# The sums along heads of a gated recurrence in two runs of five matmuls, and its last transposes twice as far apart in the plan

## The chip, the cores and the metric

The kernel runs on one core of a Trainium2 chip. A core has TensorE (PE in the profile, with its weight loads as PEld), VectorE (DVE), ScalarE (ACT), GpSimd (POOL) and SyncE (SP), which issues most of the DMAs. The metric is the device time of one execution in microseconds (us), as a median over runs.

## The reference

Two layers of a hybrid backbone are computed, one over 128 context rows and one over 512 latent rows, together 640 rows of 1024 features. Four token mixers work side by side: a short gated convolution, a gated recurrence in both directions (HGRN2), a neighbourhood attention and a chunked gMLP. A feed-forward net follows. The change touches the recurrence, which in the reference is this, for each head of 64 and for each direction:

```python
q, k, log_f, v = chunks(q), chunks(k), chunks(log_f), chunks(v)    # of 32 rows
cum = jnp.cumsum(log_f, axis=3)
rel = cum[:, :, :, :, None, :] - cum[:, :, :, None, :, :]
decay = jnp.exp(jnp.where(tri, rel, -jnp.inf))
scores = jnp.einsum('bhctd,bhcsd,bhctsd->bhcts', q, k, decay)
o_intra = jnp.einsum('bhcts,bhcsv->bhctv', scores, v)
...
def step(s, gu):
    g_c, u_c = gu
    return g_c[..., None] * s + u_c, s
s_last, s_in = lax.scan(step, s0, (g, u))
...
o = o_f + flip(o_b)
o = o * lax.rsqrt(jnp.mean(o * o, axis=-1, keepdims=True) + EPS)
return o * norm_g * silu(g), s_f, s_b
```

## The kernel before

The 640 rows are held with features along the 128 partitions. The main stream of the program is the projection of the input: for each output tile of 128 features, TensorE multiplies weights by the activations in three passes (high weight x high input, high x low, low x high). The lines are L362 (in `gemm_half`, 128x320 results) and L933 (in `tok_tile`, 128x256 results); the text calls their matmuls the main matmuls. The weights are split on the way: ACT copies the high part (L323), and DVE subtracts it from the raw weight for the low part (L324).

Everything else of the mixers runs beside that stream as jobs. A job is a Python generator that writes some instructions and then yields a number of planned microseconds. The main stream calls `tick(us)` after every three matmuls, which moves a planned clock on; each job whose due time has come then writes its next piece. `pe(us)` moves the planned clock without running a job. A yield is multiplied by the job's slack, 1.3 for the recurrence. So these numbers set where the job's matmuls stand between the main matmuls of TensorE. The framework's own scheduler then sets the order on each engine, by its estimate of when operands are there; so on DVE and ACT, and in places on TensorE, the order is not that of the code. Once fixed, each engine takes its instructions in that order.

The recurrence (`hgrn`) is computed by levels. `along` (L466) sums products over the features of a head by a matmul with a 128x2 matrix `heads`; ten such matmuls make the sums of the 640 rows and two halves, and it is called twice, once on `ksum` (in tile D) and once, at level 0, on `near` (in tile E). At each level from 1 to 6 rows are joined in blocks of twice the size:

- TensorE multiplies keys by queries in small matmuls (L526: 32x32 at levels 1 to 5, 64x64 at level 6). A level has two groups (`par` 0 and 1), at level 6 four; the queries `qq` are tile C, the keys are tile B (`kk`) or, up to level 4, copies of it in tile D or E (L493, L494).
- DVE takes the result into place under a mask (L531, up to level 4); at levels 5 and 6 ACT does it (L535). At level 4, ACT copies the four blocks of the whole to the final place (L541).
- DVE updates keys and queries with the gates: four multiplications (L545), two of tile B, then two of tile C, and one of the gates themselves (L549, tile A). The next level's matmuls read what these wrote.

After the levels the states are carried from tile to tile (L565, L574), the outputs are summed (L619 to L626) and normed (L610), and at the end they are transposed (L648), ten times in five pairs, and DVE multiplies each half by gains and gates (L652).

Other jobs in the same stretch are `gmlp`, whose norm goes by DVE (L304), GpSimd's power (L305) and five multiplications on DVE (L681); its matmuls are L686; and `ada_cols`, which makes modulation vectors on DVE (L262, two passes over 1024 elements per column, tiles H, X or A; then L228, L231 or L268).

Of the kernel before, what the change touches and what calls it, by code (L numbers as in the profile page):

```python
# [67 lines left out]
def tile_step(ctx: ExitStack, tc: tile.TileContext, a: dict, outs: list, dbg=None):  # L68
# [21 lines left out]
    def pe(us):  # L90
        now[0] += us
# [38 lines left out]
    def pm():  # L130
        return psm.tile([P, 512], F32, tag="m", name=nm("m"))
# [74 lines left out]
    for x in LORD.split():  # L206
        if x[0] == "w":
            i, h = int(x[1]), int(x[2])
# [238 lines left out]
    def hgrn():  # L447
# [13 lines left out]
        def along(x):  # L461

            m = pm()
            mv = m[:, 0:20].rearrange("p (r i) -> p i r", r=2)
            for i in range(10):
                mm(mv[:, i, :], x[:, i * P:(i + 1) * P], heads, start=True, stop=True)  # L466
                pe(0.22)
                yield 0.5
            return m


# [5 lines left out]
        for j in range(2):  # L477
            vec.tensor_tensor(n2[:, j], k2(j)[:, j], q2(1 - j)[:, 1 - j], ALU.mult)
        dm = yield from along(ksum)

        near_at = hd[:, 1280:1920].rearrange("p (r i t) -> p r i t", r=2, i=10)
# [17 lines left out]
        for l in range(7):  # L499
# [5 lines left out]
            if l == 0:  # L505
                m = yield from along(near)
                vec.copy_predicated(nat, lmask[:, 0, :].unsqueeze(1).to_broadcast([P, 20, 32]), bc(m))
# [137 lines left out]
        for t in range(5):  # L645
            m = pm()
            for pr in range(2):
                ten.transpose(m[:, pr * P:(pr + 1) * P],  # L648
                                    og[:, t * 256 + pr * P:t * 256 + (pr + 1) * P], ident)
                pe(0.11)  # L650
                s = sg[:, pr * T + t * P:pr * T + (t + 1) * P]
                vec.scalar_tensor_tensor(s, m[:, pr * P:(pr + 1) * P],  # L652
                                         p1[:, C_HN + pr:C_HN + pr + 1], s, ALU.mult, ALU.mult)
            yield 0.4
        nc.sync.dma_start(ybd, split_y("D", sg).bitcast(F32))
        R["hgrn_done"] = True
        R["yd"] = split_y("E", R["yt"])
# [1 line left out]
    def split_y(tag, y):  # L659
        w = region(tag, [P, 2, 2, T], F32R)  # L660
        wf = w.rearrange("p h k t -> p h (k t)")
        act(wf[:, 0], y, AF.Copy)
        vec.tensor_tensor(wf[:, 1], y, wf[:, 0].bitcast(F32), ALU.subtract)
        return w
# [233 lines left out]

    SLACK = {"q": 1.3, "du": 1.4, "ax": 1.0, "cv": 1.1}
    starts = {"q": hgrn, "du": gmlp, "ax": conva, "cv": attn}  # L900

    def in_tile(sec, n, w):
# [1318 lines left out]
```

## Time and profile before

| | us |
|---|---|
| median of 3 runs | 1024.82 |
| lowest and highest | 1024.57, 1025.02 |
| the profiled execution | 1023.97 |
| its span on the core | 1022.1 |
| TensorE busy | 1008.3 (99%) |
| DVE busy | 790.1 (77%) |
| ACT busy | 538.6 (53%) |
| POOL busy | 106.5 (10%) |

The profile is of one execution, and its times are microseconds from the start of the span. A row of the timeline gives start, duration, engine, line, operation, output and inputs by the names of their tiles, shapes and a count; in brackets stands the idle time of the engine just before it and what ended that. A row of waits gives who waited for whom: the sum, the number of times and the longest. A row of a window gives its length and the busy time of PE, PEld, DVE, ACT and POOL, each with a count, then the granted clock of TensorE, the share of DMA and GB/s. "x2" behind a MATMUL counts the passes that the hardware makes of an instruction on 4-byte data, two each.

### The profile page before, as it was taken

How to read it: one execution, taken by the hardware profiler on the slowest of the kernel's cores; microseconds unless marked ns; L12 is line 12 of the kernel's file. 1: busy time of each engine (PE TensorE's matmuls, PEld its weight loads, DVE VectorE, ACT ScalarE, POOL GpSimd, SP SyncE). 2: the span in 40 equal slices, each digit the busy share in tenths (PEclk: the TensorE clock that was granted, in tenths of full speed). 3: DMA queues.
4: the chain of work that ended last, by engine and by line, in shares of the span. 5: the costliest groups of instructions: out<-in, count | busy, mean ns of one | idle time of the engine just before them, and what ended most of it. 6: DMA issues, size and time to landing. Idle time of an engine off the chain costs nothing.

```text
span 1022.1 us, 18764 instructions
## 1 busy us (share of the span) xinstructions
PE 1008.3 (99%) x7572; PEld 951.9 (93%) x7572; DVE 790.1 (77%) x1308; ACT 538.6 (53%) x933; POOL 106.5 (10%) x153
## 2 busy tenths in 40 slices
PE   8999999999999999999999999999999999999997
PEld 6899999999899999999998899999999999888886
DVE  6758899769866676767868879998888887796644
ACT  6642343354555444444544567777777776634432
POOL 1000020312100000000010111111112221001101
PEclk9999999999999999999999999999999999999999
DMA  9864433597562413323179584765555669974212
GB/s 354 322 221 127 126 124 114 171 263 216 143 206 79 155 52 104 130 77 104 49 282 349 207 328 112 195 163 150 150 151 149 154 161 271 370 259 146 83 42 103
DMA packets 55926, 177.85 MB, mean 174 GB/s; under 512 B 8192, under 2 KB 14624, under 8 KB 53280
## 3 DMA queue, kind: packets, MB, share of 16 engines
q1 hardware_dynamic: 45008, 140.60, 39.6%
q0 software_dynamic: 10832, 36.06, 14.8%
q8 instruction: 59, 0.97, 0.4%
q14 instruction: 27, 0.22, 0.1%
HBM read 134.93 MB, written 25.46 MB: 157 GB/s over the span
## 4 chain that ended last, share of the span: by engine, by line
PE 91%; DVE 5%; DMA 1%; issue 1%; ACT 1%; POOL 1%; SPq 0%; POOLq 0%; DVEq 0%; ACTq 0%
PE g L1478 19%; PE m L1122 17%; PE g L362 14%; PE g L1813 8%; PE m L1813 6%; PE g L1135 5%; PE m L1478 4%; PE m L1262 3%; PE g L933 2%; PE g L1262 2%; PE m L148 2%; PE g L148 1%; PE m L1473 1%; PE m L526 1%; DMA A<-in_w_ada_dram 1%
## 5 line engine op out<-in xcount | busy, mean ns | idle before, releaser
L362 PE MATMUL g<-XH,w 128*128 128x320 f32 x704 | 171.4, 317 | 0.0
L362 PEld LDWEIGHTS g<-XH,w 128*128 128x128 f32 x704 | 120.6, 188 | 2.4 <-issue 1.2
L362 PE MATMUL g<-XL,w 128*128 128x320 f32 x352 | 108.8, 309 | 0.0
L362 PEld LDWEIGHTS g<-XL,w 128*128 128x128 f32 x352 | 66.3, 188 | 0.0
L311 DVE TENSOR_TENSOR w<-raw,w 128x1024 fp32r<-128x1024 f32 x34 | 41.4, 1221 | 14.9 <-ACT w L310 9.1
L1122 PE MATMUL m<-XH,w 128*128 128x320 f32 x224 | 52.5, 309 | 0.0
L1813 PE MATMUL g<-w,XH 128*128 128x512 f32 (+1 forms) x216 | 50.2, 385 | 0.0
L1813 PEld LDWEIGHTS g<-w,XH 128*128 128x128 f32 x216 | 39.5, 188 | 8.3 <-ACT XH L1772 0.3
L310 ACT ACTIVATE w<-raw 128x1024 fp32r<-128x1024 f32 x34 | 35.7, 1050 | 21.3 <-PE g L1262 10.0
L1813 PE MATMUL g<-w,XL 128*128 128x512 f32 (+1 forms) x180 | 42.4, 386 | 0.0
L148 DVE SCALAR_TENSOR_TENSOR X<-MG,p2t,X 128x641 f32<-128x641 f32 x44 | 38.9, 885 | 4.3 <-ACT X L148 3.4
L148 DVE SCALAR_TENSOR_TENSOR X<-X,p2t,X 128x641 f32<-128x641 f32 x44 | 38.9, 884 | 1.9 <-ACT X L148 1.0
L1813 PEld LDWEIGHTS g<-w,XL 128*128 128x128 f32 x180 | 33.4, 188 | 7.1 <-DVE dt L1828 0.2
L148 ACT ACTIVATE w<-raw 128x1024 fp32r<-128x1024 f32 (+3 forms) x46 | 38.2, 851 | 2.7 <-DMA raw<-in_w_in_dram 1.7
L1478 PE MATMUL g<-XL,w 128*128 128x320 f32 x240 | 38.6, 310 | 0.0
L1478 PE MATMUL g<-XL,C 128*128 128x320 f32 x240 | 38.4, 309 | 0.0
L1122 PEld LDWEIGHTS m<-XH,w 128*128 128x128 f32 x224 | 38.3, 188 | 0.0
L1478 PEld LDWEIGHTS g<-XL,w 128*128 128x128 f32 x240 | 36.0, 188 | 0.5 <-ACT MG L148 0.3
L1813 PE MATMUL m<-w,XH 128*128 128x512 f32 (+1 forms) x156 | 36.4, 381 | 0.0
L1478 PEld LDWEIGHTS g<-XL,C 128*128 128x128 f32 x240 | 35.9, 188 | 0.4 <-ACT MG L148 0.4
L1122 PE MATMUL m<-XL,w 128*128 128x320 f32 x112 | 34.6, 309 | 0.0
L1813 PEld LDWEIGHTS m<-w,XH 128*128 128x128 f32 x156 | 28.5, 188 | 5.6
(549 smaller groups left out, 2751.9 us busy)
## 6 DMA issues: line engine op xcount, KB each, us to landing
raw<-in_w_up_dram SPq DMA_DIRECT2D x30, 512.0 KB, 4.9
raw<-in_w_gp_dram SPq DMA_DIRECT2D x21, 640.0 KB, 4.0
raw<-in_w_down_dram SPq DMA_DIRECT2D x22, 512.0 KB, 4.0
raw<-in_w_in_dram SPq DMA_DIRECT2D x19, 512.0 KB, 4.2
H<-in_w_adt_dram SPq DMA_DIRECT2D x16, 512.0 KB, 4.5
actd<-X POOLq DMA_DIRECT2D x22, 320.5 KB, 5.4
X<-in_w_adt_dram SPq DMA_DIRECT2D x10, 512.0 KB, 4.0
upd<-XL SPq DMA_DIRECT2D x4, 1280.0 KB, 6.4
```

The costliest lines, as they stand in the source:

```text
L148: r = f(*args, **kw)
L310: act(w[0], raw, AF.Copy)
L311: vec.tensor_tensor(w[1], raw, w[0].bitcast(F32), ALU.subtract)
L362: mm(o, w[:, h, k0 + k, :], r(k)[:, s], start=(k == 0 and i == 0), stop=(k == kt - 1 and i == 2))
L526: mm(m[W * g:W * g + W, (i - s0) * W:(i - s0 + 1) * W], lhs, rhs, start=True, stop=True, tile_position=(64 * par, W * g))
L933: mm(o, x(kx)[:, ts], w[:, h, k, :], start=(kx == 0 and i == 0), stop=(kx == 7 and i == 2))
L1122: mm(o, w[:, k, :], x[:, k, :], start=(first and k == 0 and j == 0), stop=(k == 3 and j == 2), skip_group_check=True)
L1135: mm(pb[:, c, 0:HC], w[:, h + k, :], y[:, x, k, s], start=(k == 0 and j == 0), stop=(k == 1 and j == 2))
L1262: mm(m, mh[k // 2][:, hx, k % 2, t * P:(t + 1) * P], wo[q][:, hw, k % 2, :], start=(k == 0 and i == 0), stop=(k == 7 and i == 2))
L1473: mm(o, w[:, k, :], x[:, k, :], start=(first and not part and k == 0 and j == 0), stop=(part == 1 and k == 3), skip_group_check=True)
L1478: z = mm(o, w[:, k, :], x[:, k, :], start=(first and k == 0 and j == 0), stop=(k == 3 and j == 2), skip_group_check=True)
L1813: mm(ps, sl[k][hx][:, t * P:(t + 1) * P], w[:, hw, k, c0:c1], start=first, stop=end and (last or nh == 1 and t == 4 and kk_ == 7))
```

## The change

`along` yields after every fifth matmul, 2.5 planned us, and not after each, 0.5. The last transposes are 0.8 planned us apart in place of 0.4. Both are multiplied by the slack.

```diff
             for i in range(10):
                 mm(mv[:, i, :], x[:, i * P:(i + 1) * P], heads, start=True, stop=True)
                 pe(0.22)
-                yield 0.5
+                if i % 5 == 4:
+                    yield 2.5
             return m
...
                 vec.scalar_tensor_tensor(s, m[:, pr * P:(pr + 1) * P],
                                          p1[:, C_HN + pr:C_HN + pr + 1], s, ALU.mult, ALU.mult)
-            yield 0.4
+            yield 0.8
         nc.sync.dma_start(ybd, split_y("D", sg).bitcast(F32))
```

Behind L468 every line number is one higher in the changed kernel: L526 is its L527, L545 its L546 and so on. Each engine has the same instructions in both kernels. The order is the same up to the first call of `along` and again from about 223 us on; in between, it differs on every engine.

On TensorE, in the first call of `along`, the sums (L466) stand between main matmuls (L933). Before:

```order
L466 MATMUL m_1057<-heads,D_927 128x2
L933 MATMUL m_991<-w_873,XH_253 128x256 x2
L933 MATMUL m_991<-w_873,XL_15_254 128x256
L933 MATMUL m_991<-w_873,XH_253 128x256
L466 MATMUL m_1057<-heads,D_927 128x2
L933 MATMUL m_991<-w_873,XH_253 128x256
L933 MATMUL m_991<-w_873,XL_15_254 128x256
L933 MATMUL m_991<-w_873,XH_253 128x256
```

After, from the same place:

```order
L466 MATMUL m_1057<-heads,D_927 128x2 x5
L934 MATMUL m_991<-w_873,XH_253 128x256 x2
L934 MATMUL m_991<-w_873,XL_15_254 128x256
L934 MATMUL m_991<-w_873,XH_253 128x256 x2
L934 MATMUL m_991<-w_873,XL_15_254 128x256
```

The second run of five follows 19 main matmuls behind the first, and the tenth single of before 43 behind its first. In the second call the two runs stand behind 282 and 300 main matmuls, counted from the start; the ten singles stood behind 297 to 351.

On DVE, at level 4 and the updates of level 5 (128x40x16 is level 4, 128x20x32 is level 5). Before:

```order
L304 TENSOR_SCALAR dss<-dss 128x5
L545 TENSOR_TENSOR B_795<-B_795,A_794 128x40x16 x2
L681 TENSOR_SCALAR X_126_1318<-X_126_1318,dss 128x256 x2
...
L531 COPY_PREDICATED D_927<-lmask,m_1890 128x320
L545 TENSOR_TENSOR C_1008<-C_1008,A_794 128x40x16 x2
L549 TENSOR_TENSOR A_794<-A_794 128x80
L262 SCALAR_TENSOR_TENSOR junk_1942,ar_1943<-H_1529,S_94_1047 128x1024
L262 SCALAR_TENSOR_TENSOR junk_2050,ar_2051<-X_99_1078,S_94_1047 128x1024
L262 SCALAR_TENSOR_TENSOR H_1529,ar_1943<-H_1529,S_94_1047 128x1024
L324 TENSOR_TENSOR w_1964<-raw_1659,w_1964 128x1024
L228 TENSOR_SCALAR modt<-ar_1943,cst 128x2
L545 TENSOR_TENSOR B_795<-B_795,A_794 128x20x32 x2
L545 TENSOR_TENSOR C_1008<-C_1008,A_794 128x20x32 x2
```

After:

```order
L546 TENSOR_TENSOR B_795<-B_795,A_794 128x40x16
L304 TENSOR_SCALAR dss<-dss 128x5
L682 TENSOR_SCALAR X_124_1314<-X_124_1314,dss 128x256 x5
L532 COPY_PREDICATED D_927<-lmask,m_1842 128x320
L546 TENSOR_TENSOR C_1008<-C_1008,A_794 128x40x16 x2
L550 TENSOR_TENSOR A_794<-A_794 128x80
L324 TENSOR_TENSOR w_1897<-raw_1573,w_1897 128x1024
L262 SCALAR_TENSOR_TENSOR junk_1987,ar_1988<-H_1620,S_94_1047 128x1024
L262 SCALAR_TENSOR_TENSOR junk_2097,ar_2098<-X_97_1072,S_94_1047 128x1024
L262 SCALAR_TENSOR_TENSOR X_97_1072,ar_2098<-X_97_1072,S_94_1047 128x1024
L546 TENSOR_TENSOR B_795<-B_795,A_794 128x20x32 x2
L546 TENSOR_TENSOR C_1008<-C_1008,A_794 128x20x32 x2
```

The two updates of B that stood between L304 and the multiplications of L681 stand ahead of L304, and L324 stands ahead of three L262 and not behind them. On ACT the weight's high copy L323 stands behind the four copies L541 in both; the evacuation L412 between them has gone ahead of them.

On TensorE, from the last group of level 5 to the first of level 6, 30 main matmuls (L362) stand between before and 36 after. Before, the start and the end of that stretch (gmlp's L686 is in it):

```order
L526 MATMUL m_2056<-C_1008,B_795 32x32 x40
L362 MATMUL g_1969<-XH_253,w_1656 128x320
...
L686 MATMUL m_2156<-G_1983,X_126_1318 64x128 x4
L362 MATMUL g_2148<-XH_253,w_1804 128x320
L362 MATMUL g_2148<-XL_15_254,w_1804 128x320
L362 MATMUL g_2148<-XH_253,w_1804 128x320
L526 MATMUL m_2166<-C_1008,B_795 64x64 x10
```

After:

```order
L527 MATMUL m_1993<-C_1008,B_795 32x32 x40
L362 MATMUL g_1902<-XH_253,w_1570 128x320
...
L362 MATMUL g_2065<-XH_253,w_1747 128x320 x2
L362 MATMUL g_2065<-XL_16_255,w_1747 128x320
L362 MATMUL g_2065<-XH_253,w_1747 128x320
L527 MATMUL m_2106<-C_1008,B_795 64x64 x10
```

Counted from the start, the second group of level 5 stood behind 600 main matmuls and stands behind 564; the first group of level 6 stood behind 630 and stands behind 600.

The transposes L648 stood behind 822 to 840 main matmuls, at 825, 828 and 834 two at one place; they stand behind 777 to 809, at 801 two at one place. Around them on DVE, before (tile MG takes the transposes' results, D_ and E_ the split outputs):

```order
L663 TENSOR_TENSOR E_2728<-X_126_1318,E_2728 128x1280
L262 SCALAR_TENSOR_TENSOR junk_2737,ar_2738<-H_2497,S_94_1047 128x1024
L262 SCALAR_TENSOR_TENSOR H_2497,ar_2738<-H_2497,S_94_1047 128x1024
L231 TENSOR_SCALAR modt<-ar_2738,bada_240,cst 128x2
```

After, the first L652 (its L653) stands ahead of the first of these L262, and the second between the two:

```order
L653 SCALAR_TENSOR_TENSOR MG_113_1236<-m_2622,cst,MG_113_1236 128x128
L262 SCALAR_TENSOR_TENSOR junk_2746,ar_2747<-H_2554,S_94_1047 128x1024
L653 SCALAR_TENSOR_TENSOR MG_113_1236<-m_2622,cst,MG_113_1236 128x128
L653 SCALAR_TENSOR_TENSOR MG_113_1236<-m_2633,cst,MG_113_1236 128x128
L262 SCALAR_TENSOR_TENSOR H_2554,ar_2747<-H_2554,S_94_1047 128x1024
```

## The prediction

> **What bounds the kernel now.** I read the busy shares first, then the chain of work that ended last, then the waits of TensorE, then the timeline around the places that the new order touches.
>
> ```profile
> PE 1008.3 (99%) x7572; PEld 951.9 (93%) x7572; DVE 790.1 (77%) x1308; ACT 538.6 (53%) x933; POOL 106.5 (10%) x153
> PEclk9999999999999999999999999999999999999999
> PE 91%; DVE 5%; DMA 1%; issue 1%; ACT 1%; POOL 1%; SPq 0%; POOLq 0%; DVEq 0%; ACTq 0%
> PE g L148 <- DVE F L148: 1.6, 1, 1.6
> ...
> PE m L648 <- DVE MG L652: 1.0, 1, 1.0
> ```
>
> TensorE (PE) is busy 99% of the span, makes up 91% of the chain and is granted nine tenths of its clock or more in every slice. So a change pays only if it shortens the issue of TensorE or removes one of its waits, and it costs if it creates one. In the part of the program whose order changes, the only large wait is the last row: 1.0 us before a transposition of L648. VectorE (DVE) is busy 77%, but it is not idle evenly, and that is what decides below.
>
> The sum is made against the profiled execution, 1023.97 us, of which 1022.1 is the span. It lies 0.85 below the median of 1024.82, so I add the change to the median. What a measurement here can tell from no change is 0.2%, or 2.05 us.
>
> **Part 1: sums in runs of five.** No instruction is added or removed on any engine. Twenty matmuls of L466, two columns wide, stand as four runs of five. Each is cheap to compute, so what counts is how far it pushes the matmul behind it.
>
> ```profile
> 83.29 0.28 PE L466 MATMUL m<-heads,D 128*128 128x2 f32 x2
> ...
> 83.64 0.28 PE L933 MATMUL g<-w,XL 128*128 128x256 f32 x1
> 83.76 0.28 PE L933 MATMUL g<-w,XH 128*128 128x256 f32 x1
> 83.88 0.50 PE L466 MATMUL m<-heads,D 128*128 128x2 f32 x4
> ...
> 84.44 0.28 PE L933 MATMUL m<-w,XL 128*128 128x256 f32 x1
> ...
> 91.89 0.31 PE L362 MATMUL g<-XH,w 128*128 128x320 f32 x1
> 92.03 0.28 PE L466 MATMUL m<-heads,E 128*128 128x2 f32 x2
> 92.17 0.39 PE L362 MATMUL g<-XH,w 128*128 128x320 f32 x1
> 92.40 0.31 PE L362 MATMUL g<-XL,w 128*128 128x320 f32 x1
> ```
>
> Starts tell the cost. A matmul of L933 takes 0.12 (83.64 to 83.76). The single at 83.29 and its successor take 0.35 to 83.64, so the single costs 0.35 - 0.12 = 0.23. The pair at 83.88 costs 0.56 - 0.12 = 0.44, that is 0.21 for the second of it. Between matmuls of L362, which take 0.14 to 0.15, the single at 92.03 costs 0.37 - 0.15 = 0.22: 0.14 until the next starts, and 0.08 by which that next one is longer. Before, the order has two pairs and six singles in the first call of along and ten singles in the second: 0.88 + 1.38 + 2.2 = 4.5 us. After, each run costs 0.23 + 4 x 0.21 = 1.07, four of them 4.3. I take -0.1, since no run longer than two is in this trace. If the inner ones cost only the 0.14, sixteen of them save 16 x 0.08 = 1.3; if each costs what a single does, 20 x 0.23 = 4.6 make +0.1. So the bounds are -1.3 and +0.1, and the pair is the nearest row.
>
> **Part 2: the whole recurrence stands earlier.** This is the large part. Five single steps of 0.65 planned us are rounded up to the next call of tick, one step of 3.25 is rounded once. In the order that results, TensorE's steps of the recurrence come 30 to 51 main matmuls earlier at each of the levels. Counted in matmuls of L362 and L933 from the start, the first 64x64 matmuls of L526 (level 6) stand behind 630 before and behind 600 now. Behind 600 there stood before the second group of level 5:
>
> ```profile
> 145.40 0.89 PE L526 MATMUL m<-C,B 64*32 64x32 f32 x80
> 146.22 0.41 PE L362 MATMUL g<-XH,w 128*128 128x320 f32 x1
> ...
> 152.39 0.80 PE L526 MATMUL m<-C,B 64*64 64x64 f32 x20
> ```
>
> Up to that point TensorE has the same work in both orders, so it reaches the 64x64 matmuls at about 146.2 to 146.4 instead of 152.39. What they read are the two level-5 updates of C on DVE (L545). Does DVE come earlier too?
>
> ```profile
> DVE D L531 <- PE m L526: 3.0, 2, 2.2
> DVE B L545 <- PE m L526: 0.7, 1, 0.7
> DVE X L681 <- POOL dss L305: 0.3, 1, 0.3
> 105.30:149.30 44.00, 43.90 (x1049) 41.35 (x1048) 39.80 (x69) 17.96 (x37) 5.61 (x6) 1.00 0.39 122
> 105.36 1.23 DVE L324 TENSOR_TENSOR w<-raw,w 128x1024 fp32r<-128x1024 f32 x1 [1.65 <-ACT w L323]
> 132.82 0.15 DVE L304 TENSOR_SCALAR dss<-dss 128x5 f32<-128x5 f32 x1
> 132.94 1.56 DVE L545 TENSOR_TENSOR B<-B,A 128x640 f32<-128x640 f32 x2
> 134.83 0.62 DVE L681 TENSOR_SCALAR X<-X,dss 128x256 f32<-128x256 f32 x2 [0.33 <-POOL dss L305]
> 138.59 0.52 DVE L531 COPY_PREDICATED D<-lmask,m 128x320 f32<-128x320 uint8 x1 [0.79 <-PE m L526]
> 139.00 1.54 DVE L545 TENSOR_TENSOR C<-C,A 128x640 f32<-128x640 f32 x2
> 140.68 1.22 DVE L262 SCALAR_TENSOR_TENSOR junk<-H,S 128x1024 bf16<-128x1024 f32 x1
> 144.11 1.33 DVE L324 TENSOR_TENSOR w<-raw,w 128x1024 fp32r<-128x1024 f32 x1
> 146.32 1.56 DVE L545 TENSOR_TENSOR B<-B,A 128x640 f32<-128x640 f32 x2 [0.71 <-PE m L526]
> 147.80 1.55 DVE L545 TENSOR_TENSOR C<-C,A 128x640 f32<-128x640 f32 x2
> 133.05 1.75 POOL L305 TENSOR_TENSOR dss<-dss,neghalf 128x5 f32<-128x5 f32 x1 [81.91 <-DVE dss L304]
> 139.14 2.99 ACT L541 ACTIVATE MG<-D 32x640 f32<-32x640 f32 x4 [3.31 <-DVE D L531]
> ...
> 142.88 1.07 ACT L323 ACTIVATE w<-raw 128x1024 fp32r<-128x1024 f32 x1
> ```
>
> In the 44.0 us from L324 at 105.36 to the end of the level-5 updates, DVE is busy 39.8 (the third pair of the window's row) and idle about 4.0, by the three waits: 3.0 + 0.7 for TensorE and 0.3 for GpSimd (POOL). DVE's work in the stretch is nearly the same in the new order: one L262 more and one L324 less, 1.1 to 1.2 us each, and a small L228 or L268 less. With TensorE earlier, its 3.7 of idle go, and the levels would come 3.7 earlier, were there not two waits in their place:
> - L681 now stands directly behind L304. L304 hands to POOL's pow (133.05, 1.75), and L681 starts at 134.83, 1.89 after the 132.94 at which the next work could begin. Before, the two updates of B at 132.94 (1.5 together) lay in between, and 0.33 was left as a wait. In the new order both stand ahead of L304, and nothing is left in between: 1.6 more.
> - L324 now stands directly behind level 4's updates of C and L549; before, three L262 (140.68 to 144.11, 3.4) were in between. It needs L323 of ScalarE (ACT), which stands behind the four copies L541, and these wait for the second L531: 2.99 + 1.07 = 4.1 behind it. DVE has from 139.00 to 140.68 to do in that time, 1.7. So 2.1 to 2.4 idle, in place of none.
>
> Sum 1.9 + 2.1 to 2.4 = 4.0 to 4.3, against 4.0 before: DVE ends the two level-5 updates of C where it did, the second at 147.80 + 1.55 = 149.3, the first half of that span earlier, at 148.6. TensorE stands there from 146.2 or 146.4. It waits about 2.2 for the first and 0.6 for the second, 2.8 in all, and behind it in its queue stand main matmuls that need none of this. Before, the same data had 152.39 - 149.3 = 3.1 us to spare. Nothing later gives it back: TensorE has no idle time to shrink, and from 223 us on the orders are the same. Bounds: 0 if DVE's chain comes forward by 2.8 or more after all, and 4.4 if each of the two DVE waits comes out 0.8 longer. I take 2.8.
>
> The other levels have their L526 earlier too, but DVE's idle time before them (3.7) says that DVE waited for TensorE there. Small waits of 0.1 may appear at levels 2 to 4; I add 0.1.
>
> For the clock, the row of granted clock shows 9 in the slices that hold the waits of 1.6 and 1.0, so I take a wait of 2.8 at its own length. [...]
>
> **Part 3: the last transposes.** Spaced 1.04 planned us apart in place of 0.52, two of them no longer meet in one gap.
>
> ```profile
> 199.27 0.27 PE L648 MATMUL m<-cst,MG 128*128 128x128 f32 x1
> 200.56 0.33 PE L648 MATMUL m<-cst,MG 128*128 128x128 f32 x1 [1.02 <-DVE MG L652]
> ...
> 195.90 1.49 DVE L663 TENSOR_TENSOR E<-X,E 128x1280 fp32r<-128x1280 f32 x1
> ...
> 198.57 1.22 DVE L262 SCALAR_TENSOR_TENSOR H<-H,S 128x1024 f32<-128x1024 f32 x1
> 199.84 0.29 DVE L231 TENSOR_SCALAR modt<-ar,bada,cst 128x2 f32<-128x2 f32 x1
> 200.16 0.61 DVE L652 SCALAR_TENSOR_TENSOR MG<-m,cst,MG 128x128 f32<-128x128 f32 x2
> ```
>
> The second transposition waits 1.02 for L652, because DVE is in L663, two L262 and L231 until 200.16. In the new order the first L652 stands ahead of those L262, and more main matmuls stand between two transposes. I take 0.85 of the 1.02 as gone, with 0.1 to 0.2 left; bounds 0 and 1.0. The DMA behind the last L652 goes out earlier, and nobody waits for it here.
>
> **Sum:** -0.1 + 2.8 + 0.1 - 0.85 = +2.0 us (1.95). On the median, 1024.82 + 2.0 = 1026.8 us: a little slower, almost exactly at the 2.05 that can be told.
>
> **Rivals.**
> (a) The wait at level 6 does not come: DVE's chain moves forward with TensorE, because POOL's pow or ACT's L323 find other cover (the L324 buffer loaded earlier, or L304 issued earlier than I read). For it: DVE idled 3.7 for TensorE. Against it: the two rows of POOL and ACT above. It decides if no more than 1.2 of the two DVE waits is left (4.0 of idle less the 2.8 by which the chain must come forward). Then only L648's 0.85 and the 0.1 count: 1023.9.
> (b) The other side, faster: runs of five cost 0.14 for each inner matmul, -1.3, and the chain of DVE keeps up as in (a): -1.3 - 0.85 = -2.15, 1022.7. The point from which it counts as faster is 0.075 saved per inner matmul without any wait at level 6. Against it: the pair at 83.88, where the second cost 0.21.
> (c) More waits: TensorE is 30 to 51 matmuls of 0.15 (4.5 to 7.6 us) earlier at every level, and DVE turns out to be the bound at levels 3 or 4 as well, where L531 waited only 0.79. One more wait of 2 to 3: 1029.3.
> [...]
>
> **How the numbers follow.** My forecast (level 6 waits between 1.2 and 4, net +0.5 to +3.2) has 0.60, divided evenly by the bound at 2.05. (a) has 0.16, of it 0.03 on the faster side; (b) 0.12, (c) 0.09, (d) 0.03. So faster 0.15, same 0.30 + 0.13 = 0.43, slower 0.30 + 0.12 = 0.42. The range: at the low end (b) and part of (a) are left out, 1023.4, at the high end most of (c), 1028.6.
>
> **What the profile after would show.** Among TensorE's waits a new row, L527 (the old L526) on DVE's C, L546, 2 to 3 us in one or two pieces, and L649 on L653 below 0.3. On DVE a wait of L682 on POOL of 1.9 and of L324 on ACT's L323 of over 2, and nearly none on L527. Inside a run of five, starts of 0.2 apart. I am wrong if the wait at level 6 is missing or under 1 us, if the L324 directly behind L550 finds its L323 done, or if the starts inside a run are 0.14 apart.

## The result and the profile after

The changed kernel takes 1029.9 us (median of 5 runs, 1028.93 to 1034.62) against 1024.65, so by the medians it is 5.3 us slower. The ratio over all the runs, which two long ones raise, is 1.0066, with a 95% interval of 1.0051 to 1.0081. The forecast was 1026.8, with a range of 1023.4 to 1028.6.

The five runs fall into two groups: 1028.93, 1029.09 and 1029.9, and 1033.45 and 1034.62. The profiled execution is of the second group (1033.45 us, a span of 1031.6). Its page, in the rows that answer to those of before:

```profile
PE 1015.8 (98%) x7572; PEld 957.4 (93%) x7572; DVE 789.2 (77%) x1308; ACT 538.5 (52%) x933; POOL 112.1 (11%) x153
PEclk9999999999999999999999999999999999999999
PE 77%; issue 9%; DVE 6%; DMA 4%; ACT 1%; POOL 1%; SPq 0%; POOLq 0%; DVEq 0%; ACTq 0%
```

TensorE fell from 91% of the chain to 77%. "issue" went from 1% to 9%, and DVE and DMA gained 4 points together. The row of granted clock shows no dip, because a slice is 25.8 us long and the dip lies across two of them. A window of 15 us does. Its row, with the clock third from the end:

```profile
145.00:160.00 15.00, 13.73 (x120) 12.18 (x118) 10.83 (x19) 4.55 (x10) 0.97 (x1) 0.66 0.33 108
```

Windows of 1 us show 1.00 up to 149 us, 0.50 from 150 to 159 us and 1.00 from 160 us on, so a mean of 0.66 over 15 us is (1 - 0.66) x 15 / 0.5 = 10.2 us at half clock, and about 5 us are lost. The waits of TensorE between 76 and 240 us, and below them the timeline where the clock falls:

```profile
PE m L649 <- DVE MG L653: 2.2, 2, 1.3
PE m L527 <- DVE C L546: 1.3, 2, 0.9
PE g L934 <- issue: 0.2, 1, 0.2
```

```profile
147.00 0.31 PE L362 MATMUL g<-XH,w 128*128 128x320 f32 x1
148.17 0.33 PE L527 MATMUL m<-C,B 64*64 64x64 f32 x2 [0.86 <-DVE C L546]
148.91 0.79 PE L527 MATMUL m<-C,B 64*64 64x64 f32 x18 [0.41 <-DVE C L546]
149.63 0.63 PE L362 MATMUL g<-XH,w 128*128 128x320 f32 x1
```

The wait at level 6 is there (0.86 + 0.41 idle; by starts 0.93 + 0.63, about 1.6), and the first main matmul behind it takes 0.63 in place of 0.41. The transposes wait 2.2 us in place of 1.0. (By the counts of the traces, L466 and L527 have two rows for each matmul of the code, x20 for the ten of a call. Main matmuls and transposes have one, so there "x2" is two matmuls, the main ones 0.15 us apart.)

### The profile page after: what moved, and what is told of

It reads as the page before. It is cut to its first block, busy times and chain, and to the rows that moved or that the text cites. A ratio compares the mean times of both kernels' runs of the same rounds, so it can differ in the third digit from the quotient of the medians.

```text
span 1031.6 us, 18766 instructions
## 1 busy us (share of the span) xinstructions
PE 1015.8 (98%) x7572; PEld 957.4 (93%) x7572; DVE 789.2 (77%) x1308; ACT 538.5 (52%) x933; POOL 112.1 (11%) x153
## 4 chain that ended last, share of the span: by engine, by line
PE 77%; issue 9%; DVE 6%; DMA 4%; ACT 1%; POOL 1%; SPq 0%; POOLq 0%; DVEq 0%; ACTq 0%
PE g L1479 19%; PE m L1123 17%; PE g L362 8%; PE g L1814 8%; PE m L1814 5%; PE g L1136 5%; PE m L1479 4%; PE m L1263 3%; PE g L1263 2%; DMA hdr<-MG 1%; PE m L1474 1%; DVE junk L262 1%; DMA A<-in_w_ada_dram 1%; PE m L148 1%; DVE D L586 1%
## 5 line engine op out<-in xcount | busy, mean ns | idle before, releaser
L362 PE MATMUL g<-XH,w 128*128 128x320 f32 x704 | 172.3, 321 | 0.0
L362 PEld LDWEIGHTS g<-XH,w 128*128 128x128 f32 x704 | 122.3, 191 | 2.6 <-issue 1.2
L362 PE MATMUL g<-XL,w 128*128 128x320 f32 x352 | 110.4, 314 | 0.0
L362 PEld LDWEIGHTS g<-XL,w 128*128 128x128 f32 x352 | 67.5, 192 | 0.1
L310 ACT ACTIVATE w<-raw 128x1024 fp32r<-128x1024 f32 x34 | 35.7, 1051 | 22.1 <-PE g L1263 10.2
L323 ACT ACTIVATE w<-raw 128x1024 fp32r<-128x1024 f32 (+1 forms) x22 | 24.3, 1103 | 20.5 <-issue 9.1
```

Of the source, the lines that this page charges most:

```text
L310: act(w[0], raw, AF.Copy)
L323: high = lambda: act(w[:, 0], raw, AF.Copy)
L362: mm(o, w[:, h, k0 + k, :], r(k)[:, s], start=(k == 0 and i == 0), stop=(k == kt - 1 and i == 2))
```

## The experiments

Each comparison is with the kernel before, run on the same chip (medians of 1024.3 to 1024.5). Time lost is read as the start of the same main matmul in both traces, or as the distance of two starts less what the same pair takes before.

**The changed kernel again.**

> The changed kernel once more. Theory 1 (the level-6 wait lowers the clock): the executions fall into two groups, near 1029 with a mean granted clock of 0.998 and near 1034 with 0.993; if the profiled one is of the second group, the clock is 0.5 for about 10 us from the level-6 matmuls on, and if it is of the first, it is 1.0 there and the waits of 1.5 us at level 6 and 2.5 us at the transposes are the same. Rival (a disturbance that has nothing to do with the wait): half clock shows at another place or in no run, and all runs lie near 1029.

Measured: 1028.87 us (1028.38 to 1031.36), ratio 1.0046 (1.0033 to 1.0058). Four runs lie at 1028.4 to 1029.5 and one at 1031.36 with a clock of 0.996. The profiled one has the full clock at level 6, so it shows the loss without the dip. Its waits in the same stretch, and the window of 15 us from 145 on:

```profile
PE m L649 <- DVE MG L653: 2.1, 2, 1.3
PE g L934 <- issue: 0.7, 1, 0.7
PE m L527 <- DVE C L546: 0.4, 1, 0.4
PE m L527 <- issue: 0.2, 1, 0.2
145.00:160.00 15.00, 14.57 (x165) 12.28 (x163) 13.67 (x25) 7.08 (x16) 0.94 (x1) 1.00 0.39 112
```

Two main matmuls of the kernel before, and then the timeline of TensorE in this run at the places that cost, with the same two at its end:

```profile
189.62 0.31 PE L362 MATMUL g<-XL,w 128*128 128x320 f32 x1
...
224.90 0.46 PE L362 MATMUL g<-XH,w 128*128 128x320 f32 x2
```

```profile
108.51 0.28 PE L934 MATMUL g<-w,XH 128*128 128x256 f32 x1
...
109.47 0.39 PE L934 MATMUL g<-w,XH 128*128 128x256 f32 x1 [0.68 <-issue]
...
148.15 0.32 PE L527 MATMUL m<-C,B 64*64 64x64 f32 x2
148.88 0.79 PE L527 MATMUL m<-C,B 64*64 64x64 f32 x18 [0.41 <-DVE C L546]
...
192.69 0.31 PE L362 MATMUL g<-XL,w 128*128 128x320 f32 x1
...
229.44 0.46 PE L362 MATMUL g<-XH,w 128*128 128x320 f32 x2
```

So 192.69 - 189.62 = 3.1 us are lost up to the end of the outputs, and 4.5 behind the transposes; the rest of the program keeps it (the last matmul is 4.4 late). Of the 3.1, about 0.8 is the gap at 108.51 (0.96 in place of 0.12), 0.3 a second issue wait within L527 at 124, and 0.7 level 6. The remaining 1.3 are small pieces, 0.25 of them behind the two calls of `along`; what made the other 1.0 stays open. The transposes cost 1.4 more than before. The level-6 wait is smaller here than in the first trace (0.7 in place of 1.6) since TensorE came later by the larger issue wait: the two together are 1.8 and 1.9.

The queue of VectorE explains the transposes. Of the timeline, the issue of a load (SPq), VectorE's rows and the transposes that wait:

```profile
193.34 0.33 SPq L248 DMA_DIRECT2D H<-in_w_adt_dram  x1
...
193.69 1.22 DVE L262 SCALAR_TENSOR_TENSOR junk<-A,S 128x1024 bf16<-128x1024 f32 x1
...
196.48 0.35 DVE L653 SCALAR_TENSOR_TENSOR MG<-m,cst,MG 128x128 f32<-128x128 f32 x1
...
196.89 0.33 PE L649 MATMUL m<-cst,MG 128*128 128x128 f32 x1 [0.85 <-DVE MG L653]
...
198.38 1.22 DVE L262 SCALAR_TENSOR_TENSOR junk<-H,S 128x1024 bf16<-128x1024 f32 x1 [1.55 <-DMA H<-in_w_adt_dram]
...
199.53 0.60 DVE L653 SCALAR_TENSOR_TENSOR MG<-m,cst,MG 128x128 f32<-128x128 f32 x2
...
200.19 0.33 PE L649 MATMUL m<-cst,MG 128*128 128x128 f32 x1 [1.28 <-DVE MG L653]
```

The first L653 stands behind two L262 of tile A, and the second behind an L262 of tile H. The load of H is issued at 193.34, and that L262 starts at 198.38. VectorE does nothing for 1.55 us ahead of it, and TensorE, which stops at 198.9, then waits for the product queued behind it.

**Each part alone.** The runs of five alone, with 0.4 at the transposes:

```diff
-            yield 0.8
+            yield 0.4
```

> Only the runs of five; the last transposes 0.4 planned us apart as before. Theory 1: the level-6 wait of 1.5 us and with it the two groups of runs stay; theory 2 (the wait at the transposes comes from the whole chain being earlier, so that VectorE's queue stands at L262 and a late load): L649 still waits 2 to 3 us, and the time is that of the changed kernel, 1028.5 to 1029.5 without the half clock. Rival (the spacing of 0.8 makes the wait at the transposes): it waits 1.1 or less there, and the time is 1027 to 1028.

Measured: 1043.21 us, 1.0185 (1.0171 to 1.0198). Up to the first transposes its order is that of the changed kernel, and up to 240 us its waits are too (2.2 us at the transposes, 1.2 at level 6), so the spacing did not make the wait at the transposes. The rest lies behind it, where the order differs from before up to 280 us on TensorE and some 300 on VectorE and ScalarE:

```profile
PE m L865 <- DVE B L1932: 3.6, 1, 3.6
PE g L362 <- ACT gt L972: 3.2, 1, 3.2
```

Neither theory had this. The 0.8 delays the end of the recurrence in the plan, and with it the later order falls back to that of before. Half of the change repairs some 14 us of damage of the other half. Some 5 of these 14 are clock: the trace is of the one run at 0.997, 1038.31 us, and the others have 0.992.

The spacing alone, on the kernel before (0.4 to 0.8):

> Only the spacing of 0.8; the sums singly as before. By part 3 of the prediction the wait of 1.1 us at the transposes goes or is below 0.3: 1023.6 to 1024.0. Rival (the spacing itself costs, since the transposes reach further): the wait stays at 1 us or more, 1024.6 to 1026. No half clock in any run by either.

Measured: 1025.77 us, ratio 1.0007 (0.9999 to 1.0016). The wait stays, and between 195 and 260 us another grows (0.2, once, in the kernel before):

```profile
PE m L847 <- DVE X L844: 1.2, 2, 0.7
PE m L648 <- DVE MG L652: 1.0, 1, 1.0
```

My part 3 is refuted by this: the transposes are further apart, and the second still waits for VectorE's L663, two L262 and L231, which end when they did. Alone, the spacing gains nothing: the median lies 1.25 us above 1024.52, with an interval that still holds 1, and the 1.2 us at L847 come near that.

**Level 6 later**, in the changed kernel:

```diff
-            yield HD[1]
+            yield HD[1] + (2 if l == 5 else 0)
...
-        yield HY
+        yield HY - 2
```

> The changed kernel with level 6 two planned us later (its first matmuls behind 618 main matmuls in place of 600) and the transposes two planned us less behind the outputs. Theory 1: no wait at level 6 (0 to 0.3 us), so no execution shows half a clock and all lie together; the transposes wait as in the changed kernel, 1.5 to 3 us: 1027 to 1028. Rival (a disturbance of its own): one or two of the executions still are 5 us longer at a clock of 0.993.

Measured: 1028.58 us, 1.0038 (1.0026 to 1.0051). No wait at level 6 is left, but one of 2.1 us at the transposes (waits, and a window of 10 us):

```profile
PE m L649 <- DVE MG L653: 2.1, 1, 2.1
```

```profile
195.00:205.00 10.00, 8.21 (x48) 8.06 (x49) 8.18 (x21) 1.89 (x3) 2.53 (x3) 0.83 0.90 238
```

The clock of 0.83 over 10 us is 3.4 us at half clock; they begin at 198.1, 1.3 us behind the end of that wait. So both were half right: in this trace the level-6 dip went with the level-6 wait, and executions still differ (clocks of 0.995 to 0.999), since a dip can stand behind another wait.

**No product between the transposes of a pair**, in the changed kernel:

```diff
             for pr in range(2):
                 ten.transpose(m[:, pr * P:(pr + 1) * P], ..., ident)
                 pe(0.11)
+            for pr in range(2):
                 s = sg[:, pr * T + t * P:pr * T + (t + 1) * P]
```

> The changed kernel, where both transposes of a pair are issued ahead of both products of VectorE, so that no transposition waits for L653. Theory 2 (VectorE's queue, which stands at L262 for a late load, costs 2.5 us at the transposes): the waits of L649 on L653 fall from 2.2 us to under 0.3, and the time by 2.0 to 2.5, to 1026.3 to 1027.0. Rival (the queue is late in any case and the wait goes to the next user of its results): less than 1 us is gained, 1028 or more.

In the code a product stands between the two transposes of a pair, whose results are two halves of one tile, and in the traces the second transposition waits for that product. Measured: 1027.2 us, 1.0041 (1.0024 to 1.0057), 1.7 less than 1028.87; by the distances from each one's own kernel before (2.9 and 4.35) it is 1.4. At least 2.0 was expected. The wait falls from 2.1 to 0.6:

```profile
PE m L527 <- DVE C L546: 0.9, 2, 0.5
PE m L649 <- DVE MG L654: 0.6, 1, 0.6
PE g L935 <- issue: 0.6, 1, 0.6
```

That the waits at the transposes are VectorE's queue, and cost about what they measure (1.5 us less of wait), is shown.

**The levels back at their place**, in the changed kernel, without and with that pairing:

```diff
-        yield HD[0]
+        yield HD[0] + 5
```

> The changed kernel with five planned us more ahead of the first level, so that the levels, the outputs and the first transposition stand behind the same number of main matmuls as before (426 to 636, 672 to 726, 822). The runs of five and the spacing of 0.8 stay. Theory 3 (the loss comes from the levels standing earlier and not from the runs of five): no wait at level 6, no half clock, 1 to 1.3 us of wait at the transposes as before, and the time is that of before within 1 us, 1023.8 to 1025.3. Rival (the runs of five or the spacing cost by themselves): 1026 to 1029.

> As levels_back, and both transposes of a pair ahead of both products. Theories 2 and 3 together: no wait at level 6 nor at the transposes, about 1 us less than the kernel before: 1022.8 to 1024.0. Rival (a wait at the transposes only moves on): 1024.5 or more.

Measured: 1026.93 us, 1.0027 (1.0017 to 1.0038), and with the pairing 1024.35 us, 1.0003 (0.9993 to 1.0013). Without the pairing:

```profile
PE m L649 <- DVE MG L653: 1.1, 1, 1.1
PE g L362 <- issue: 0.7, 1, 0.7
PE m L848 <- DVE X L845: 0.4, 1, 0.4
```

The level-6 wait is gone and 2 of the 4.4 us are back, less than theory 3 expected. An issue wait stays, now at 122.6 us, and the waits of L848 for L845 come to 1.1 us up to 260 us, as with the spacing alone. With the pairing it is as fast as before but no faster, although the transposes no longer wait. Its trace has issue waits of 1.1 and 1.0 us, but it is of the slowest of ten runs (1028.35 us, with 3.4 us at half clock behind one of them); that such waits take the gain in the median run too is not shown. Theory 3 holds for level 6 only.

**The four copies on GpSimd**, in the changed kernel:

```diff
-                    act(at[c, :, :, c].rearrange("p r i t -> p (r i) t"), nat[c], AF.Copy)
+                    pool.tensor_copy(at[c, :, :, c].rearrange("p r i t -> p (r i) t"), nat[c])
```

> The changed kernel with the four copies of level 4 (L541, here L542) on GpSimd in place of ScalarE; VectorE's order up to level 6 is the same but for one small L228. Step of the prediction (L324 waits for L323, which stands behind the four copies): L323 runs 3 us earlier, the wait of 2.5 us of L324 falls under 0.5, and the level-6 matmuls wait under 0.3 in place of 0.7 to 1.5; the waits at the transposes stay, and the time is 1027 to 1028. Rival (another wait of VectorE takes its place, or the load of the weights is late): the level-6 wait stays and the time is 1028.5 or more.

Measured: 1028.12 us, 1.0041 (1.0027 to 1.0056). L324 in the changed kernel, and then in this one, with what follows it:

```profile
140.87 1.23 DVE L324 TENSOR_TENSOR w<-raw,w 128x1024 fp32r<-128x1024 f32 x1 [2.49 <-ACT w L323]
...
147.31 1.55 DVE L546 TENSOR_TENSOR C<-C,A 128x640 f32<-128x640 f32 x2
```

```profile
138.29 1.22 DVE L324 TENSOR_TENSOR w<-raw,w 128x1024 fp32r<-128x1024 f32 x1
...
140.57 1.73 DVE L262 SCALAR_TENSOR_TENSOR junk<-X,S 128x1024 bf16<-128x1024 f32 x1
...
142.35 1.61 DVE L262 SCALAR_TENSOR_TENSOR X<-X,S 128x1024 f32<-128x1024 f32 x1
...
146.47 1.55 DVE L546 TENSOR_TENSOR C<-C,A 128x640 f32<-128x640 f32 x2
```

The wait for L323 is gone, so its cause is shown. The level-6 wait was expected under 0.3, and that failed. But the updates of C come only 0.84 earlier, not 2.5: two of the three L262 take 1.6 to 1.7 in place of 1.2 to 1.3 while GpSimd copies (9.1 us in all, from 136.8), the updates of B are longer too (2.07 in place of 1.64), and L228 moved ahead of them. TensorE still waits 0.7 at level 6.

**The places of the code packets.** The trace has a queue that carries only instructions, on the page of every run:

```profile
q8 instruction: 59, 0.97, 0.4%
```

0.97 MB / 59 = 16.4 KB each. In the second trace of the changed kernel one such packet is under way from 106.8 to 107.9 us; the issue wait ends at 109.47, 1.5 later. So I moved them, by 32 more small matmuls at the start (WARM 100 to 132), and spread the dense matmuls of level 1:

```diff
-                    yield 3 if l == 4 else 0.4
+                    yield 3 if l in (1, 4) else 0.4
...
-            yield HD[1]
+            yield HD[1] - (2.6 if l == 1 else 0)
```

> The changed kernel with 32 more of the small matmuls that warm TensorE at the start (about 0.05 us each), all else in the same order; they move the places in TensorE's instruction stream at which its 16 KB code packets end. Theory 4 (the waits called issue, 0.3 to 0.8 us at 108.5 and 0.3 at 124 us, are TensorE waiting for its next code packet behind the dense level matmuls): they disappear there or move to another place by several us. Rival (they belong to the work at that place): they stay between the same two matmuls, as in all four traces of this order so far. The time is within 1.5 us of the changed kernel by either.

> The changed kernel with the two groups of level 1 some 20 main matmuls apart in place of 3; the end of level 1 keeps its planned time. Theory 4: with the dense matmuls spread, the issue wait at 108.5 us goes (under 0.1), and none takes its place there. Rival: 0.3 us or more of issue wait stay between 105 and 112 us. The time is 1027 to 1030 by either, since the waits at the transposes stay.

Measured: 1030.47 and 1030.59 us, one run each; both traces have 3.4 us at half clock behind an issue wait, and the second has 3.4 more at the transposes. With 32 more, the wait between the two L934 is gone and two others stand inside the level matmuls, at 108.9 and 137.7 (waits, and the timeline at the first):

```profile
PE m L527 <- issue: 2.1, 2, 1.3
```

```profile
106.80 0.72 PE L527 MATMUL m<-C,D 64*32 64x32 f32 x60
108.85 0.38 PE L527 MATMUL m<-C,D 64*32 64x32 f32 x20 [1.33 <-issue]
```

With level 1 spread, none is left at 105 to 112, and one of 1.2 stands in L527 at 122. There the packets land at 107.5 and 121.8, and the waits end 1.3 and 1.5 later.

Counting settles where these waits stand. Take all of TensorE's instructions in a trace in the order of their starts: matmuls, weight loads and its own semaphore instructions. The issue waits over 0.15 us between 76 and 240 us, twelve in eight traces, stand only in front of number 2242, 2754, 3009 or 3522, which are whole multiples of 256 apart (3009 is one short). With 32 more matmuls at the start the wait moved to other work and kept its number, 2242. So it belongs to a place in the instruction stream and not to the work. All twelve end 1.3 to 1.5 us after a packet landed. Give the k-th packet to the k-th such place, 256 apart; then in none of the fourteen traces does TensorE pass one, with a wait or without, sooner than 1.2 us after its packet landed. So the late packet is what these waits fit in every case. No run moved a packet alone. Dense groups by themselves are not enough: the kernel before has groups as dense (x80 at 143.95 and at 145.40 us, also 3 main matmuls apart) and no such wait.

**Level 6 earlier still** (1.5 planned us, the transposes as much later):

> The changed kernel with level 6 a further 1.5 planned us earlier (its first matmuls behind 585 main matmuls in place of 600) and the transposes as much later. The waits at level 6 grow to some 2.5 to 3.3 us in 4 us. [...] Rival (the clock falls by chance): some runs at 1030 to 1031 with a clock of 0.998.

Measured: 1032.6 us (1030.94 to 1037.56, 4 runs), 1.0087 (1.0064 to 1.011). The profiled one (1033.9), by its waits and two windows:

```profile
PE m L649 <- DVE MG L653: 2.7, 1, 2.7
PE m L527 <- DVE C L546: 2.5, 2, 2.1
```

```profile
145.00:160.00 15.00, 12.59 (x122) 11.49 (x122) 12.16 (x22) 4.81 (x11) 0.54 (x1) 0.77 0.32 105
200.00:210.00 10.00, 7.27 (x41) 6.65 (x40) 6.61 (x18) 0.79 (x1) 2.42 (x3) 0.83 0.82 239
```

That is 6.9 and 3.4 us at half clock behind its two waits. The rival asked for runs with a clock of 0.998, and there is none: the four have 0.992 to 0.997. Four runs, one of them traced, do not tell whether such a wait lowers the clock always or only more often.

**The pairing on the kernel before:**

> The kernel before, where both transposes of a pair are issued ahead of both products. Theory 2: the wait of 1.0 us of L648 on L652 goes, and nothing takes its place: 1.0 to 1.3 us less than before, 1022.9 to 1023.4 where before has 1024.3. Rival (the wait moves on to the next user of VectorE's results): within 0.4 us of before.

Measured: 1023.02 us (1022.47 to 1024.14, 11 runs), 0.9986 (0.9977 to 0.9995). TensorE has no wait over 0.15 us between 76 and 240 us in its trace. It is the one version here that beats both kernels, by 1.3 us of the one before.

## Why the prediction was wrong

The sign was right and the size was not: 1.95 us were forecast, 4.4 came without the half clock and 5.3 in the first median. The steps that failed are the transposes, put at a gain, and the issue waits and the clock, put at nothing. In the second trace, which is 4.5 us late behind the transposes, the terms measure: the calls of `along` 0.25 (forecast -0.1), issue waits 1.1 (not in the sum), level 6 0.7 (2.8), the transposes 1.4 (-0.85) and small pieces 1.0 (0.1). So the right sign is in part luck: the term that gave it makes 0.7 of the 4.5.

- **Runs of five (-0.1).** Right in what a matmul of a run costs: inner starts are 0.22 apart. By the first main matmul of L934 behind both calls, 103.73 against 103.48, 0.25 us are lost, over the bound of +0.1; 0.17 of it stand at one place, 84.9 us, and not within a run. What I did not price is that the same code, placed otherwise, meets other ends of code packets: issue waits of 0.2 to 2.1 us in eight of the eleven traces with runs of five, none in the three without.
- **Level 6 (+2.8).** The mechanism was right, row by row: L324 waits 2.49 for L323 (forecast 2.1 to 2.4), the wait for GpSimd is 1.3 (1.9), and the second update of C ends at 147.31 + 1.55 = 148.9 (149.3). The term was too large because TensorE came at 147.1 to 148.0 and not at 146.2 to 146.4: it had lost 0.7 to 1.8 us on the way, to issue waits and small waits. It measured 1.6 and 0.7.
- **The clock.** I gave 0.03 to (d), a loss of clock behind the wait, on the ground that a wait of 1.6 and one of 1.0 showed no dip. It is what separates the groups of runs, as far as their clocks are on record, and it cost about 5 us in the first trace. The row that I read could not have shown it, since ten microseconds at half clock in the trace after still print as 9s. The reading itself was true, as finer windows of before show the full clock at those transposes (1.00 from 195.5 to 206 us); but one execution without a dip says little of the next.
- **The transposes (-0.85).** This step failed, in sign too: +1.4. I read the order up to the first L653 and not what stood ahead of it (two L262 of tile A) and behind it (an L262 whose load was issued 5 us earlier). I had also asked of VectorE's L262 only how long they take and not when their loads land; moved 45 matmuls earlier, the transposes met a load in flight.
- **Nothing later.** Right for the change, whose order is that of before from 223 us on (on VectorE from 232). The runs of five alone show how near it was: +18.7 us.

In these traces the stretches at half clock come out at 3.4, 6.9 and 10.2 us. The one of the first trace lasts 10.24 us, 149.64 to 159.88, which is 3 x 3.413, and in the run with level 6 earlier still the two begin at 149.84 and 204.45, 16 x 3.413 apart. In the first trace 0.86 + 0.41 us of idle time, with small matmuls between, left TensorE busy for 2.14 of the 3.41 us ahead of the dip. The runs of five alone have 0.83 + 0.41 there, 2.17 us busy in as long a stretch, and the full clock behind it. So what decides about a dip stays open.

## What to carry to other kernels

When a planner's numbers move a chain earlier on the engine that bounds, ask at each place where it is waited for what the slower engine has queued ahead, its loads included, and whether its data come earlier at all. An instruction of another engine between two of the bounding engine's is worth moving by itself: it gave 1.3 us to the kernel before and 1.4 to 1.7 to the changed one. And test the parts of such a change singly and together: here one part alone cost 18.7 us, and the other, which alone gained nothing, was its repair.

## What the hardware showed

- TensorE's clock fell to half (0.50 in windows of 1 us) for 3.4 us or a multiple, behind or at the end of waits that come to 1.0 to 3.2 us, in some executions of the same program only. With one such dip the time of a variant varies by 2 to 5 us between runs, which is as much as the change moved.
- In places TensorE waited for no operand but, by all that the traces show, for its own instructions. At dense small matmuls (two groups of x80 in the trace, with their weight loads, within 3 main matmuls) stand waits of 0.2 to 1.3 us, twelve in eight traces, always at places a multiple of 256 instructions apart, that end 1.3 to 1.5 us after a packet of instructions landed (0.97 MB / 59 = 16.4 KB each).
- While GpSimd copied for 9 us, two of three L262 of VectorE took 1.6 to 1.7 us in place of 1.2 to 1.3; the first of them took 1.22 as ever. No run here separates the copies from what moved with them.
